# Mixer of a hybrid decoder step: state buffers, turning of the values and head norms rearranged

## The chip, the cores and the metric

The kernel runs on one core of a Trainium2 chip. The metric is the device time of one execution in microseconds (us), lower is better. A core has five engines that work side by side, each through its own list of instructions in order: TensorE (PE, matrix products into PSUM banks; its weight loads are listed as PEld), VectorE (DVE), ScalarE (ACT), GpSimd (POOL) and SyncE (SP, which here only issues transfers). Transfers between the memory (HBM) and the core's buffers (SBUF) are issued by SP or POOL.

## The reference

One inference step of a decoder layer with d = 2048, for a prompt of 256 tokens and 8 samples of 4 tokens each (together T = 288 columns):

```python
x = x + 0.5 * rmsnorm(swiglu(rmsnorm(x, g[0]), ffn1_w_in, ffn1_w_out), g[1])
m, sg, sh = hybrid_mixer(rmsnorm(x, g[2]), ...)
x = x + rmsnorm(m, g[3])
x = x + 0.5 * rmsnorm(swiglu(rmsnorm(x, g[4]), ffn2_w_in, ffn2_w_out), g[5])
```

The mixer projects its input with one matrix into the parts of a GLA group (4 heads, key width 128, value width 256) and an HGRN group (8 heads, 128 and 128). Each head runs the recurrence S_t = diag(a_t) S_{t-1} + k_t^T v_t, o_t = q_t S_t, from zero for the prompt and from a given state for each sample. Each head's output is normalised (rmsnorm), multiplied by silu of a gate, and all heads go through the output projection. The outputs are the new tokens' values, and the states of the prompt and of the samples. Everything is float32.

## The kernel before

The three sub-layers follow each other: FFN1, mixer, FFN2. Activations are kept with features on the 128 partitions and the 288 tokens along the free dimension; a feature tile is 128 x 288. For precision every product is made of three matmuls: a weight is split into wh (ScalarE's rounded copy, L86) and wl (VectorE's rest, L87), an activation into xh and xl, and TensorE adds wh xh (L464), wh xl (L465) and wl xh (L466).

`block` (L455) makes 512 output features: four feature tiles f = 0..3, each with a PSUM bank of its own, over 16 slices k of the input; 192 matmuls in all. After each slice it calls `tick(k)`, which issues a piece of other work into the same in-order lists of the engines; the program's order is the engines' order. The last slices are done tile by tile, and after each tile `evac` takes the bank off. The blocks of the mixer run in the order qk0, v0, qk1, v1 (GLA queries and keys, values, for two pairs of heads), hfq0, hi0, hfq1, hi1, hfq2, hfq3 (HGRN forget gates and queries; values), gate0 to gate3, and the output projection mo0 to mo3.

What `tick` issues comes from generators. `scan` (L764) is one for a pair of heads: eight levels of scores, after which `out`, `final`, `halve`, `sample`, `inter_a`, `inter_b` and `norm_a` follow one step at a time. It holds:
- the samples' states, loaded by SP in `load_state` (L783) into a ring "s0" of four buffers, split by `halve` (L942) into halves hl on ScalarE and VectorE, updated in `sample` (L954) on VectorE (L973) and stored by POOL (L975). A load waits for the store that held its buffer. SP's list holds the loads of weights (L61, L63) and of states in one order;
- the head norm: `norm_a` squares (hsq; the sum of two halves is GpSimd's, L998), `norm_b` (L1006) forms the mean in a scratch bank hms on TensorE, one step later `norm_c` (L1011) takes the inverse root. The list `later` holds how many steps each of these comes behind.

Values are needed with tokens on the partitions. `ev_v` (L741) multiplies a value tile by the row factor into vt (L744, L745), and at once transposes it on TensorE (tp_v, L727 and L728) and copies it to three places (L751, L752, L732 and L734). Such transposes, the scores (sc), out (o, os), sn, st and hms all take their PSUM bank from one ring of three (`auxtile`); the main products have the other five.

`ev_hgrn` (L1114) makes the forget gate, its key k and q from a feature tile z (two buffers) with ScalarE's Exp and Ln; the key's way goes through a tile mx. `ev_gate` (L1170) makes the gate, and for gate0 and gate1 multiplies y by z on GpSimd (L1179).

Of the kernel before, what the change touches and what calls it, by code (L numbers as in the profile page):

```python
# [16 lines left out]
P = 128  # L17
# [98 lines left out]
def trunk_kernel(ctx, tc, x_prompt, x_sample, state_gla, state_hgrn, norm_gains, f1_in, f1_out, f2_in, f2_out,  # L116
# [540 lines left out]
    def mixer(pn, border):  # L657
        with ExitStack() as mx:
# [5 lines left out]
            def scan_pool():  # L664
                border.pools.close()
                sp.append(mx.enter_context(tc.tile_pool(name="scan", bufs=2, side="right", reuse_waits="tile")))
                for i in range(2):
                    its2.append(sp[0].tile([P, 256], F32, name=f"it{i}", bufs=1))
                    vs32.append(sp[0].tile([P, 512], F32, name=f"vs{i}", bufs=1))

                    qm.append(sp[0].tile([P, 9 * 64], F32R, name=f"qm{i}", bufs=1))
            ones = {dv: cst.tile([P, P], F32R, name=f"ones{dv}") for dv in (256, 128)}
            mk = cst.tile([P, 576], U8, name="mk")
            bmask = cst.tile([96, NB], F32, name="bmask")

            sel = cst.tile([P, TS], F32, name="sel")
            its2, vs32, qm = [], [], []
# [7 lines left out]
            def setup():  # L685
# [8 lines left out]
                for t in (*its2, *vs32):  # L694
                    G.memset(t, 0.0)
# [14 lines left out]
                G.tensor_copy(bmask, bm32)  # L710
                for dv in (256, 128):
                    S.activation(ones[dv], onesD, AF.Copy, scale=float(D // dv))
# [28 lines left out]
            def ev_v(Vt, V32, Vs):  # L741
                def ev(f, ps):
                    vt = tmp.tile([P, TP + 96], F32, name="vt", tag="vt")
                    V.tensor_tensor(vt[:, 0:TP], ps[:, 0:TP], rt[:, 0:TP], op=ALU.mult)  # L744
                    V.tensor_tensor(vt[:, TP:].rearrange("p (n t) -> p n t", n=3),  # L745
                                    ps[:, TP:T].unsqueeze(1).broadcast_to([P, 3, TS]),
                                    rt[:, TP:T].unsqueeze(1).broadcast_to([P, 3, TS]), op=ALU.mult)
                    tp = auxtile("tp_v")
                    by_token(tp, vt, vt[:, TP:])
                    c = slice(f * P, (f + 1) * P)  # L750
                    S.activation(Vt[:, 0:2, c], tp[:, 0:TP].rearrange("p (t c) -> p t c", c=P), AF.Copy)  # L751
                    S.activation(V32[0:TS, c], tp[0:TS, TP:TP + P], AF.Copy)  # L752
                    stack(Vs[:, c], tp, TS)
                return ev
# [9 lines left out]
            def scan(d, Vt, V32, Vs, gla, ytile0, s0, sp_out, ss_out):  # L764
# [18 lines left out]
                def load_state():  # L783
                    if loads:
                        a, b0 = loads.pop(0)
                        t = sp[0].tile([P, nb, dv], F32, name="s0", tag="s0", bufs=4)
                        nc.sync.dma_start(t, s0[b0:b0 + nb, a].rearrange("b p v -> p b v"))
                        states[a, b0] = t
# [81 lines left out]
                for step in range(LEVELS + 1):  # L870
# [19 lines left out]
                    if step >= LEVELS - 2:  # L890
                        load_state()
                    yield
                put(LEVELS - 1, pss.pop(LEVELS - 1))
                kds, bds, hls, its, sqs, pos, mss = {}, {}, {}, {}, {}, {}, {}
# [82 lines left out]
                def inter_a(a):  # L977
                    ss = pos[a][1]
                    its[a] = it = its2[a]
                    S.activation(it[0:2 * TS, 0:dv], ss[0:2 * TS, 0:dv], AF.Copy)  # L980
                    if not gla:
                        V.tensor_tensor(it[0:2 * TS, 0:dv], it[0:2 * TS, 0:dv], ss[0:2 * TS, dv:2 * dv], op=ALU.add)

                def inter_b(a):
                    for j in range(nv):
                        c0 = TP + j * TS
                        PE.matmul(pos[a][1][:, c0:c0 + TS], its[a][:, j * P:(j + 1) * P], sel, start=False, stop=True,
                                  skip_group_check=True)

                def norm_a(a):  # L990
                    for j in range(nv):
# [5 lines left out]
                        if j == 1:  # L997
                            G.tensor_tensor(sq, sq, sqs[a], op=ALU.add)  # L998
# [12 lines left out]
                def norm_c(a):  # L1011
                    r0 = tmp.tile([P, T], F32, name="r0", tag="lsg")
                    r1 = tmp.tile([P, T], F32, name="r1", tag="ls")
                    m = tmp.tile([P, T], F32, name="hm", tag="mx")
                    V.tensor_scalar(m, mss[a][:, 0:T], EPS, None, op0=ALU.add)
                    act(r0, m, AF.Ln)
                    act(r0, r0, AF.Exp, scale=-0.5)

                    V.tensor_tensor(r1, r0, r0, op=ALU.mult)
                    V.scalar_tensor_tensor(r1, r1, -0.5, m, op0=ALU.mult, op1=ALU.mult)  # L1020
                    V.scalar_tensor_tensor(r1, r1, 1.5, r0, op0=ALU.add, op1=ALU.mult)
                    for j in range(nv):
                        yt = y[ytile0 + a * nv + j]
                        gcol = prm[:, 108 + j:109 + j] if gla else prm[:, 110:111]
                        V.scalar_tensor_tensor(yt, yt, gcol, r1, op0=ALU.mult, op1=ALU.mult)
# [8 lines left out]
                for a in range(2):  # L1034
# [19 lines left out]
                    later.append([lambda: None, lambda a=a: norm_b(a), lambda a=a: norm_c(a)])  # L1054
# [7 lines left out]
            def tick(k=None):  # L1062

                due = list(later)
                step(k)
# [48 lines left out]
            def ev_hgrn(d, g):  # L1114
                def ev(f, ps):
# [9 lines left out]
                    m = tmp.tile([P, T], F32, name="mx", tag="mx")  # L1125

                    V.tensor_tensor(m, ls, z, op=ALU.subtract)
                    act(m, m, AF.Exp)
                    act(ls, ls, AF.Exp)
                    V.tensor_scalar(d["k"][:, f, :], m, omlb[:, hd:hd + 1], None, op0=ALU.mult)  # L1130
# [21 lines left out]
            for kind, g in HORDER:  # L1152
                if kind == "hi":
                    written(g)
                    vts[g] = vtiles(f"h{g}")
                    block(f"hi{g}", KT, xrhs, ev_v(*vts[g]), tick=tick)
# [13 lines left out]
            def ev_gate(n):  # L1170
                def ev(f, ps):
# [3 lines left out]
                    if n < 2:  # L1175
# [3 lines left out]
                        G.tensor_tensor(y[t], y[t], z, op=ALU.mult)  # L1179
# [96 lines left out]
```

## Time and profile before

| | us |
|---|---|
| three runs | 2312.02, 2314.31, 2318.01 (median 2314.31) |
| profiled execution | 2314.71 |
| its span | 2312.9 |
| TensorE busy | 2291.0 (99%) |
| VectorE, ScalarE, GpSimd busy | 1421.2, 1012.7, 64.4 |
| mixer in the span | 856 to 1448 |
| TensorE's granted clock, mean | 0.997 |

The page gives for each engine the time in which it worked and its share of the span. A group of instructions is written as line, engine, operation, out<-in. A line of waits names who waited, for whom, and then the total, the number of times and the longest, in us. The chain follows the work that ended last back from one instruction to the one that released it; its lines are start, duration and what. Times inside the span are us from its start. The granted clock is the share of full speed at which TensorE was allowed to run.

### The profile page before, as it was taken

The numbers are of one execution on the slowest core, as the hardware profiler recorded it, in microseconds if no ns is written. First come the engines' busy times: TensorE is split into PE (matmuls) and PEld (weight loads), VectorE is DVE, ScalarE is ACT, GpSimd is POOL, SyncE is SP. The second block draws the span as 40 slices with busy tenths as digits, with TensorE's granted clock in tenths as the row PEclk, the third lists the DMA queues.
The fourth block names the chain that finished last, engine by engine and source line by source line (L and its number), as shares of the span: only waits on it lengthen the run. The fifth ranks groups of instructions, "written<-read, shape, count | busy, mean of one in ns | idle before, by whom it ended". The sixth has DMA issues, their size and how long they took to land.

```text
span 2312.9 us, 42140 instructions
## 1 busy us (share of the span) xinstructions
PE 2291.0 (99%) x17352; PEld 2276.1 (98%) x17352; DVE 1421.2 (61%) x2314; ACT 1012.7 (44%) x1555; POOL 64.4 (3%) x110
## 2 busy tenths in 40 slices
PE   9999999999999999999999999999999999999998
PEld 8999999999999999999999999999999999999998
DVE  7545545554556568787889854854555555545545
ACT  6443333333334446454555554544333333333345
POOL 0000000000000001001001100100000000000000
PEclk9999999999999999999999999999999999999999
DMA  7555555555555545555555555455555555555553
GB/s 214 164 166 164 165 166 168 168 165 164 167 167 186 157 151 159 152 152 171 149 169 156 159 184 167 129 160 172 165 165 167 169 164 163 165 164 166 165 164 115
DMA packets 217008, 378.16 MB, mean 163 GB/s; under 512 B 15362, under 2 KB 52400, under 8 KB 216816
## 3 DMA queue, kind: packets, MB, share of 16 engines
q1 hardware_dynamic: 211264, 365.48, 52.6%
q0 software_dynamic: 3376, 9.81, 1.3%
q8 instruction: 136, 2.23, 0.4%
q10 hardware_dynamic: 2176, 0.18, 0.1%
q14 instruction: 56, 0.46, 0.1%
HBM read 363.62 MB, written 11.80 MB: 162 GB/s over the span
## 4 chain that ended last, share of the span: by engine, by line
PE 94%; DVE 3%; issue 1%; DMA 1%; ACT 1%; POOL 0%; DVEq 0%; SPq 0%; POOLq 0%; ACTq 0%
PE gate L465 9%; PE gate L466 9%; PE gate L464 9%; PE out L465 8%; PE out L466 8%; PE out L464 8%; PE up L466 8%; PE up L464 8%; PE up L465 8%; PE hfq L464 2%; PE hfq L465 1%; PE mo L466 1%; PE mo L464 1%; PE mo L465 1%; PE hfq L466 1%; PE sc L830 1%
## 5 line engine op out<-in xcount | busy, mean ns | idle before, releaser
L87 DVE TENSOR_TENSOR wl<-raw,wh 128x1024 fp32r<-128x1024 f32 (+1 forms) x674 | 821.1, 1219 | 629.1 <-ACT wh L86 626.5
L86 ACT ACTIVATE wh<-raw 128x1024 fp32r<-128x1024 f32 (+1 forms) x674 | 711.3, 1056 | 1073.3 <-PE gate L465 323.9
L465 PE MATMUL gate<-xl,wh 128*128 128x288 f32 x1660 | 489.2, 295 | 0.2 <-DVE xl L243 0.2
L464 PE MATMUL gate<-xh,wh 128*128 128x288 f32 x1660 | 488.4, 296 | 0.7 <-DVE z L1174 0.5
L466 PE MATMUL gate<-xh,wl 128*128 128x288 f32 x1660 | 488.7, 295 | 0.2 <-DVE wl L87 0.2
L465 PE MATMUL out<-hl,wh 128*128 128x288 f32 x1408 | 415.8, 295 | 0.0
L464 PE MATMUL out<-hh,wh 128*128 128x288 f32 x1408 | 415.6, 295 | 0.0
L466 PE MATMUL up<-xh,wl 128*128 128x288 f32 x1408 | 415.0, 295 | 0.0
L466 PE MATMUL out<-hh,wl 128*128 128x288 f32 x1408 | 415.0, 295 | 0.0
L464 PE MATMUL up<-xh,wh 128*128 128x288 f32 x1408 | 414.6, 294 | 0.3 <-DVE g L523 0.3
L465 PE MATMUL up<-xl,wh 128*128 128x288 f32 x1408 | 414.8, 295 | 0.0
L465 PEld LDWEIGHTS gate<-xl,wh 128*128 128x128 f32 x1660 | 311.7, 188 | 1.1 <-DVE xl L243 1.0
L464 PEld LDWEIGHTS gate<-xh,wh 128*128 128x128 f32 x1660 | 310.5, 188 | 1.6 <-DVE z L1174 0.7
L466 PEld LDWEIGHTS gate<-xh,wl 128*128 128x128 f32 x1660 | 311.4, 188 | 0.7 <-DVE wl L87 0.7
L466 PEld LDWEIGHTS out<-hh,wl 128*128 128x128 f32 x1408 | 264.7, 188 | 0.0
L464 PEld LDWEIGHTS up<-xh,wh 128*128 128x128 f32 x1408 | 264.1, 188 | 0.6 <-DVE g L523 0.5
L464 PEld LDWEIGHTS out<-hh,wh 128*128 128x128 f32 x1408 | 264.6, 188 | 0.0
L465 PEld LDWEIGHTS out<-hl,wh 128*128 128x128 f32 x1408 | 264.5, 188 | 0.0
L466 PEld LDWEIGHTS up<-xh,wl 128*128 128x128 f32 x1408 | 264.2, 188 | 0.1
L465 PEld LDWEIGHTS up<-xl,wh 128*128 128x128 f32 x1408 | 264.2, 188 | 0.1
L583 DVE TENSOR_TENSOR y<-out,y 128x288 f32<-128x288 f32 x288 | 121.4, 452 | 104.5 <-PE out L466 101.7
L464 PE MATMUL hfq<-xh,wh 128*128 128x288 f32 x256 | 78.7, 307 | 0.0
(342 smaller groups left out, 2581.6 us busy)
## 6 DMA issues: line engine op xcount, KB each, us to landing
raw<-in_ffn_w_in_dram SPq DMA_DIRECT2D x352, 512.0 KB, 3.6
raw<-in_ffn_w_out_dram SPq DMA_DIRECT2D x176, 512.0 KB, 3.7
raw<-in_mix_w_in_dram SPq DMA_DIRECT2D x64, 512.0 KB, 3.7
raw<-in_mix_w_in_dram SPq DMA_DIRECT2D x96, 256.0 KB, 3.3
raw<-in_mix_w_out_dram SPq DMA_DIRECT2D x32, 512.0 KB, 3.8
out_dram<-s POOLq DMA_DIRECT2D x32, 256.0 KB, 3.3
s<-in_state_gla_dram SPq DMA_DIRECT2D x16, 256.0 KB, 3.6
s<-in_state_hgrn_dram SPq DMA_DIRECT2D x16, 256.0 KB, 3.4
```

The lines of the kernel that those rows point to most:

```text
L86: i1 = self.nc.scalar.activation(h[:, c], raw[:, c], AF.Copy).ins
L87: i2 = self.nc.vector.tensor_tensor(l[:, c], raw[:, c], h[:, c].bitcast(F32), op=ALU.subtract).ins
L464: yield lambda: PE.matmul(dst, w[0][:, c:c + P], parts[0], start=start, stop=False)
L465: yield lambda: PE.matmul(dst, w[0][:, c:c + P], parts[1], start=False, stop=False)
L466: yield lambda: PE.matmul(dst, w[1][:, c:c + P], parts[0], start=False, stop=stop)
L583: V.tensor_tensor(y[k], ps, y[k], op=ALU.add)
L830: PE.matmul(ps[0:m, c:c + 64], k[:, a, i * P:i * P + m], r, start=c == 0, stop=True, skip_group_check=True)
```

## The change

Five things, all in the mixer:
- The ring of state buffers "s0" has five buffers, not four, and the loads begin one step earlier (from step LEVELS-3), so they run four ahead. To make place, the two tiles `it` become one, and mx is gone: `ev_hgrn` works in place in z.
- The transposes of the values are no longer issued by `ev_v` itself. It keeps vt in a tile of y that is not yet in use (y[8..11], for hi1 y[12..15]), its samples' part in a small tile v3 (four buffers), and appends a function `turn` to a list. `tick` pops one per step, ahead of the scan's step, except at k = 0. For v0 all four come in qk1's steps 1 to 4; for v1, hi0 and hi1 two come in the block's own last two steps and two in the next block's steps 1 and 2.
- The head norm's `norm_b` and `norm_c` come one step later.
- `norm_c` has a new form: Ln takes EPS as its bias, the square of the inverse root is ScalarE's, and the factor -0.5 lies in a gain made once (hgain). VectorE has two operations per head fewer, ScalarE one more, and the bank hms is read until VectorE's first product.
- The sum of hsq and y times z go from GpSimd to VectorE.

```diff
@@ -664,17 +664,18 @@
             def scan_pool():
                 border.pools.close()
                 sp.append(mx.enter_context(tc.tile_pool(name="scan", bufs=2, side="right", reuse_waits="tile")))
+                its.append(sp[0].tile([P, 256], F32, name="it", bufs=1))
                 for i in range(2):
-                    its2.append(sp[0].tile([P, 256], F32, name=f"it{i}", bufs=1))
                     vs32.append(sp[0].tile([P, 512], F32, name=f"vs{i}", bufs=1))
 
                     qm.append(sp[0].tile([P, 9 * 64], F32R, name=f"qm{i}", bufs=1))
             ones = {dv: cst.tile([P, P], F32R, name=f"ones{dv}") for dv in (256, 128)}
             mk = cst.tile([P, 576], U8, name="mk")
             bmask = cst.tile([96, NB], F32, name="bmask")
+            hgain = cst.tile([P, 3], F32, name="hgain")
 
             sel = cst.tile([P, TS], F32, name="sel")
-            its2, vs32, qm = [], [], []
+            its, vs32, qm = [], [], []
 
             aw, alr = y[KT - 2:], y[KT - 3]
             ahl = gp.tile([P, 32 * KT + 96], F32R, name="ahl", tag="V")
@@ -691,7 +692,7 @@
                 G.dma_start(bm32, masks[0:96, 576:584])
                 for t in (*aw, alr):
                     G.memset(t, 0.0)
-                for t in (*its2, *vs32):
+                for t in (*its, *vs32):
                     G.memset(t, 0.0)
                 for g in range(2):
                     for i in range(2):
@@ -708,6 +709,7 @@
                     G.memset(qm[a].bitcast(F32), 0.0)
                 V.tensor_tensor(sel, ident[:, 0:TS], ident[:, TS:2 * TS], op=ALU.add)
                 G.tensor_copy(bmask, bm32)
+                V.tensor_scalar(hgain, prm[:, 108:111], -0.5, None, op0=ALU.mult)
                 for dv in (256, 128):
                     S.activation(ones[dv], onesD, AF.Copy, scale=float(D // dv))
 
@@ -738,19 +740,26 @@
                 return (gp.tile([P, 2, 512], F32, name=f"V{nm}", tag="V"), vs32[-1],
                         gp.tile([96, 512], F32R, name=f"Vs{nm}", tag="Vs"))
 
-            def ev_v(Vt, V32, Vs):
+            turns = []
+
+            def ev_v(Vt, V32, Vs, y0=8):
                 def ev(f, ps):
-                    vt = tmp.tile([P, TP + 96], F32, name="vt", tag="vt")
+
+                    vt = y[y0 + f]
+                    v3 = tmp.tile([P, 3, TS], F32, name="v3", tag="v3", bufs=4)
                     V.tensor_tensor(vt[:, 0:TP], ps[:, 0:TP], rt[:, 0:TP], op=ALU.mult)
-                    V.tensor_tensor(vt[:, TP:].rearrange("p (n t) -> p n t", n=3),
-                                    ps[:, TP:T].unsqueeze(1).broadcast_to([P, 3, TS]),
+                    V.tensor_tensor(v3, ps[:, TP:T].unsqueeze(1).broadcast_to([P, 3, TS]),
                                     rt[:, TP:T].unsqueeze(1).broadcast_to([P, 3, TS]), op=ALU.mult)
-                    tp = auxtile("tp_v")
-                    by_token(tp, vt, vt[:, TP:])
-                    c = slice(f * P, (f + 1) * P)
-                    S.activation(Vt[:, 0:2, c], tp[:, 0:TP].rearrange("p (t c) -> p t c", c=P), AF.Copy)
-                    S.activation(V32[0:TS, c], tp[0:TS, TP:TP + P], AF.Copy)
-                    stack(Vs[:, c], tp, TS)
+
+                    def turn():
+                        tp = auxtile("tp_v")
+                        by_token(tp, vt, v3.rearrange("p n t -> p (n t)"))
+                        c = slice(f * P, (f + 1) * P)
+                        S.activation(Vt[:, 0:2, c], tp[:, 0:TP].rearrange("p (t c) -> p t c", c=P), AF.Copy)
+                        S.activation(V32[0:TS, c], tp[0:TS, TP:TP + P], AF.Copy)
+                        stack(Vs[:, c], tp, TS)
+
+                    turns.append(turn)
                 return ev
 
             def log_sigmoid(out, z):
@@ -783,7 +792,7 @@
                 def load_state():
                     if loads:
                         a, b0 = loads.pop(0)
-                        t = sp[0].tile([P, nb, dv], F32, name="s0", tag="s0", bufs=4)
+                        t = sp[0].tile([P, nb, dv], F32, name="s0", tag="s0", bufs=5)
                         nc.sync.dma_start(t, s0[b0:b0 + nb, a].rearrange("b p v -> p b v"))
                         states[a, b0] = t
 
@@ -887,11 +896,11 @@
                             S.activation(mh, qa, AF.Copy)
                             V.tensor_tensor(ml, qa, mh.bitcast(F32), op=ALU.subtract)
                             S.activation(K3[:, a], k[:, a, TP:T].unsqueeze(1).broadcast_to([P, 3, TS]), AF.Copy)
-                    if step >= LEVELS - 2:
+                    if step >= LEVELS - 3:
                         load_state()
                     yield
                 put(LEVELS - 1, pss.pop(LEVELS - 1))
-                kds, bds, hls, its, sqs, pos, mss = {}, {}, {}, {}, {}, {}, {}
+                kds, bds, hls, sqs, pos, mss = {}, {}, {}, {}, {}, {}
 
                 def key_t(a):
                     tp = auxtile("tp_k")
@@ -976,7 +985,7 @@
 
                 def inter_a(a):
                     ss = pos[a][1]
-                    its[a] = it = its2[a]
+                    it = its[0]
                     S.activation(it[0:2 * TS, 0:dv], ss[0:2 * TS, 0:dv], AF.Copy)
                     if not gla:
                         V.tensor_tensor(it[0:2 * TS, 0:dv], it[0:2 * TS, 0:dv], ss[0:2 * TS, dv:2 * dv], op=ALU.add)
@@ -984,7 +993,7 @@
                 def inter_b(a):
                     for j in range(nv):
                         c0 = TP + j * TS
-                        PE.matmul(pos[a][1][:, c0:c0 + TS], its[a][:, j * P:(j + 1) * P], sel, start=False, stop=True,
+                        PE.matmul(pos[a][1][:, c0:c0 + TS], its[0][:, j * P:(j + 1) * P], sel, start=False, stop=True,
                                   skip_group_check=True)
 
                 def norm_a(a):
@@ -995,7 +1004,7 @@
                         sq = sqp.tile([P, T], F32, name="hsq", tag="sq")
                         S.activation(sq, yt, AF.Square)
                         if j == 1:
-                            G.tensor_tensor(sq, sq, sqs[a], op=ALU.add)
+                            V.tensor_tensor(sq, sq, sqs[a], op=ALU.add)
                         sqs[a] = sq
                     h = sqp.tile([P, T], F32R, name="nh", tag="pn")
                     l = sqp.tile([P, T], F32R, name="nl", tag="pn")
@@ -1011,18 +1020,16 @@
                 def norm_c(a):
                     r0 = tmp.tile([P, T], F32, name="r0", tag="lsg")
                     r1 = tmp.tile([P, T], F32, name="r1", tag="ls")
-                    m = tmp.tile([P, T], F32, name="hm", tag="mx")
-                    V.tensor_scalar(m, mss[a][:, 0:T], EPS, None, op0=ALU.add)
-                    act(r0, m, AF.Ln)
+                    act(r0, mss[a][:, 0:T], AF.Ln, bias=epst)
                     act(r0, r0, AF.Exp, scale=-0.5)
 
-                    V.tensor_tensor(r1, r0, r0, op=ALU.mult)
-                    V.scalar_tensor_tensor(r1, r1, -0.5, m, op0=ALU.mult, op1=ALU.mult)
-                    V.scalar_tensor_tensor(r1, r1, 1.5, r0, op0=ALU.add, op1=ALU.mult)
+                    S.activation(r1, r0, AF.Square)
+                    V.scalar_tensor_tensor(r1, mss[a][:, 0:T], EPS, r1, op0=ALU.add, op1=ALU.mult)
+                    V.scalar_tensor_tensor(r1, r1, -3.0, r0, op0=ALU.add, op1=ALU.mult)
                     for j in range(nv):
                         yt = y[ytile0 + a * nv + j]
-                        gcol = prm[:, 108 + j:109 + j] if gla else prm[:, 110:111]
-                        V.scalar_tensor_tensor(yt, yt, gcol, r1, op0=ALU.mult, op1=ALU.mult)
+                        V.scalar_tensor_tensor(yt, yt, hgain[:, j:j + 1] if gla else hgain[:, 2:3], r1,
+                                               op0=ALU.mult, op1=ALU.mult)
 
                 tp = key_t(0)
                 halve(0, 0)
@@ -1051,7 +1058,7 @@
                     yield
                     inter_b(a)
                     norm_a(a)
-                    later.append([lambda: None, lambda a=a: norm_b(a), lambda a=a: norm_c(a)])
+                    later.append([lambda: None, lambda: None, lambda a=a: norm_b(a), lambda a=a: norm_c(a)])
                     yield
                     if a == 0:
                         out(1)
@@ -1062,6 +1069,8 @@
             def tick(k=None):
 
                 due = list(later)
+                if turns and k != 0:
+                    turns.pop(0)()
                 step(k)
                 for f in due:
                     f.pop(0)()
@@ -1122,12 +1131,11 @@
                         V.scalar_tensor_tensor(d["q"][:, f - 2, :], z, QSCALE, ls, op0=ALU.mult, op1=ALU.mult)
                         return
                     hd = 2 * g + f
-                    m = tmp.tile([P, T], F32, name="mx", tag="mx")
-
-                    V.tensor_tensor(m, ls, z, op=ALU.subtract)
-                    act(m, m, AF.Exp)
+
+                    V.tensor_tensor(z, ls, z, op=ALU.subtract)
+                    act(z, z, AF.Exp)
                     act(ls, ls, AF.Exp)
-                    V.tensor_scalar(d["k"][:, f, :], m, omlb[:, hd:hd + 1], None, op0=ALU.mult)
+                    V.tensor_scalar(d["k"][:, f, :], z, omlb[:, hd:hd + 1], None, op0=ALU.mult)
                     V.tensor_scalar(d["f"][:, f, :], ls, omlb[:, hd:hd + 1], lb[:, hd:hd + 1], op0=ALU.mult, op1=ALU.add)
                 return ev
 
@@ -1153,7 +1161,7 @@
                 if kind == "hi":
                     written(g)
                     vts[g] = vtiles(f"h{g}")
-                    block(f"hi{g}", KT, xrhs, ev_v(*vts[g]), tick=tick)
+                    block(f"hi{g}", KT, xrhs, ev_v(*vts[g], 8 + 4 * g), tick=tick)
                 else:
                     written(g)
                     ds[g] = group_tiles(f"h{g}")
@@ -1176,7 +1184,7 @@
                         s = tmp.tile([P, T], F32, name="lsg", tag="lsg")
                         log_sigmoid(s, z)
                         act(s, s, AF.Exp)
-                        G.tensor_tensor(y[t], y[t], z, op=ALU.mult)
+                        V.tensor_tensor(y[t], y[t], z, op=ALU.mult)
                     else:
                         s = z
                         act(z, z, AF.Silu)
```

## The prediction

> **What bounds the kernel now.** I read the page's busy table first, then the groups of matmuls, then the waits of TensorE, and last the chain, the waits and the clock of the one stretch where TensorE stood longest.
>
> ```profile
> PE 2291.0 (99%) x17352; PEld 2276.1 (98%) x17352; DVE 1421.2 (61%) x2314; ACT 1012.7 (44%) x1555; POOL 64.4 (3%) x110
> L464 PE MATMUL hfq<-xh,wh 128*128 128x288 f32 x256 | 78.7, 307 | 0.0
> ```
>
> TensorE (PE) is the bound from end to end; VectorE (DVE) at 61% and ScalarE (ACT) at 44% have room as averages, and GpSimd (POOL) does almost nothing. A matmul of 128x288 is listed with some 295 to 307 ns, but they overlap: in the chain below one follows the other every 0.13 us (132 ns). The change removes no matmul, so all that it can take away is time in which TensorE waits or runs slowly:
>
> ```profile
> PE tp_prm L269 <- DMA stage<-in_norm_gains_dram: 4.7, 1, 4.7
> PE tp_v L728 <- DVE vt L745: 3.3, 1, 3.3
> PE pre L353 <- DVE acc L326: 0.7, 2, 0.5
> PE sc L830 <- DVE k_h L813: 0.7, 1, 0.7
> PE hms L1009 <- ACT nh L1002: 0.5, 1, 0.5
> PE gate L464 <- DVE z L1174: 0.5, 1, 0.5
> PE tp_v L727 <- DVE vt L744: 0.4, 1, 0.4
> PE tp_v L727 <- DVE Vsg L734: 0.3, 1, 0.3
> ```
>
> Columns: total, times, longest, in us. The first and third are outside the mixer and stay. The others, 5.7 us, are all at places that the change touches. The 3.3 us is one event, at the border from block hi0 to block hfq1. The chain there:
>
> ```profile
> 1061.48 3.52 DMA out_dram<-s
> ...
> 1065.02 3.44 DMA s<-in_state_hgrn_dram
> ...
> 1068.50 1.05 ACT wh L86
> ...
> 1069.57 1.23 DVE wl L87
> 1070.80 0.18 DVE vt L745
> ...
> 1071.02 0.45 PE tp_v L728
> ```
>
> Read it upwards: the transpose of the values waits for vt, which stands in VectorE's order behind the rounding rest wl of a weight, that behind ScalarE's wh, and wh stands in ScalarE's order behind the copy hl of a state that had not landed; the state's load had waited for a buffer that an older state's store still held. The waits of 1050 to 1075 us agree:
>
> ```profile
> ACT hl L950 <- DMA s<-in_state_hgrn_dram: 5.9, 2, 3.0
> DVE wl L87 <- ACT wh L86: 5.8, 2, 3.6
> ```
>
> And what comes after the stop (columns: stretch, length, busy of PE, PEld, DVE, ACT, POOL, granted clock, DMA share, GB/s):
>
> ```profile
> 1066.00:1071.00 5.00, 1.73 (x14) 1.50 (x12) 1.43 (x4) 1.67 (x3) 0.00 (x0) 0.93 0.56 174
> 1071.00:1078.00 7.00, 6.98 (x35) 6.93 (x36) 4.79 (x14) 3.95 (x15) 0.95 (x1) 0.57 0.65 187
> 1078.00:1085.00 7.00, 7.00 (x64) 6.74 (x63) 6.18 (x15) 2.70 (x7) 0.13 (x1) 1.00 0.07 10
> ```
>
> In the 7 us behind the stop TensorE is busy throughout but was granted 0.57 of its clock: 35 matmuls where the next 7 us hold 64. That is 7 x 0.43 = 3.0 us lost on top of the wait.
>
> **The change, part by part.** Sum against the profiled execution, 2314.71 us (span 2312.9 and 1.8 around it), 0.4 us above the median of 2314.31. Stalls are counted from start to start of TensorE's instructions in the trace, as excess over the same pair elsewhere, so they come out some tenths above the listed waits. 0.3%, about what a measurement of this kernel can tell from no change, is 6.9 us.
>
> *The stop at 1071 us (five state buffers, turns later).* It takes 3.45 us of wait and 3.0 us of half clock, 6.45 us. In the new order ScalarE still has wh behind the copy of the second HGRN state. But with a fifth buffer that load waits for the store before the one it waited for: that store landed at 1061.1 us, the one waited for now at 1062.1. So the load takes the place in SP's queue of the first HGRN load, issued at 1061.2 and landed at 1064.1 (2.9 us), where the second was issued at 1062.2 and landed at 1068.1 (5.9 us). Then three copies hl and it (0.3 us apart), wh 1.05 us to about 1066.2, wl 1.23 us to about 1067.5, and the two halves of the value's product (0.41 and 0.25 us) to about 1068.0; the last main matmul of hi0 is at 1067.6. Left: about 0.4 us, without a clock loss, as stops of under 1 us show none (below). Gain 6.05 us. If the load still takes 5.9 us, the stop stays as it is: gain 0. If there were no wait at all, 6.45. I take 6.05: 2.9 us is the row of the load issued at that time.
>
> The queues passed: SP issues the HGRN loads one place earlier, ahead of weight loads (hgrn1 before the weights that it followed). The weights behind a load that waits for its buffer wait as well; the store that hgrn1 needs landed at 1051.6 us, so it doesn't block, and the pair of weights behind hgrn2 and hgrn3 goes out at about 1063 as before. POOL's stores are moved past nothing.
>
> *The border v1 to hfq0, 993 to 999 us.* Three stops: 0.61 us (tp_v for vt), 0.48 us (tp_v for its bank, held by Vsg), 0.70 us (hms for nh): 1.79 us. The first two come from ScalarE, which at 986.0 to 989.8 us stands 3.9 us for a state's load, with the copy hl (0.40), wh (0.96), wl (1.23) and vt (0.34) in line behind. With the fifth buffer this load is issued several us earlier. The hms stop ends with hsq on POOL (1.35 us) and nh (0.45 us); one step more is 12 main matmuls, 1.6 us, over twice the stop. I leave 0.2 us: gain 1.6 (0 to 1.8).
>
> *Gates, 1259.0, 1293.8 and 1297.0 us.* 0.88 us (sc for k), 0.67 us (the next gate's bank for z on VectorE) and 0.30 us (hms). There POOL's y x z takes 0.80 to 1.0 us, once 3.06 us, and VectorE's products beside it take 0.92 and 1.06 us against 0.44 alone. On VectorE y x z costs 0.44 us each, 8 x 0.44 = 3.5 us in all, less than the slowed neighbours cost. The order of TensorE's instructions also puts the score about 8 and the gate's next block about 7 main matmuls later (0.9 us). Gain 0.9 + 0.9 = 1.8 us (0 to 1.85).
>
> *Head norms.* 12 heads lose two VectorE operations each (hm and the square, 24 x 0.45 = 10.8 us busy) and give ScalarE one Square (12 x 0.43 = 5.2 us); the four adds of hsq come to VectorE (4 x 0.41 us) with the eight y x z. Net VectorE -5.7 us of 1421, ScalarE +5.2 of 1013. Neither is on the path: 0, hidden by TensorE's main matmuls (192 in a block, 25.4 us). If the cover is gone one norm costs its own 0.4 us.
>
> *What is new.* The gate z is now overwritten in place, so its buffer is held through two exponentials until k is made, about 1.3 us longer than when mx took it; the third feature tile's z needs the buffer of the first, and frees the bank that the next block wants. The bank of hfq3's fourth tile is claimed at 1187.64 us, 0.08 us after z frees one: no slack. By the order of VectorE's work I put 0.15 us at hi0, 0.3 at hfq3, 0.3 at gate0. The four turns of hi1 now share three scratch banks with out and sn at the start of hfq2: 0.1. Together 0.85 us; bounds 0 (the tenths are free) and 4 x 0.88 = 3.5 us (the dearest short stop of the trace at each of the four).
>
> Sum: -6.05 - 1.6 - 1.8 + 0.85 = -8.6 us: 2314.71 - 8.6 = **2306.1 us**.
>
> **A rule weighed.** The trace's row: a stop of 3.45 us, then 6.1 us at half the clock; the stops of 0.3 to 0.9 us were followed by none. The Trainium skill, "TensorE: Matmul & The Clock Gate", section "Part 1: The HAM clock gate", says that the clock halves after an idle window of about 3.4 us which runs free of the kernel. By that rule 3.45 us would only just, and in few executions, hold a whole window, so that some runs before had no loss; after the change nothing that long is left in the mixer and the forecast time is the same by rule and by row. The lowest run of before, 2312.02 us, is 2.7 us below the profiled one, which would fit. The gain against such a run would be 5.6 us.
>
> **The rivals.**
> - *The load stays slow (0.15).* Loads and stores of 256 KB took 2.5 to 5.9 us to land; around 1063 to 1069 us the queue holds two stores, three state loads and two weights. If hgrn2 again takes 5.9 us, TensorE stands about 3.1 us and loses the 3.0 us as now: 2306.1 + 6.05 = 2312.2 us. For it: the same transfers still collide. Against: the load issued at 1061.2 took 2.9.
> - *The half clock stays (0.08).* If it comes from something other than the stop: 2306.1 + 3.0 = 2309.1 us. Against: no other place in the mixer shows it.
> - *The short stops stay (0.10).* Of the 3.4 us at v1 and the gates nothing goes, as other work in the same in-order queues takes the place: 2309.5 us. That the fifth buffer and the later turns do nothing there belongs here.
> - *Slower: scratch banks (0.12).* An hms bank is now held until VectorE's first product, with Ln, Exp and Square (3 x 0.43 us) on ScalarE before it, possibly behind one wh (1.06) and two hl (2 x 0.36), and that product (0.45) behind one wl (1.22): 4.7 us. There are three banks; a third claim after hms comes about two steps later, 3.2 us. TensorE would then stand 1.5 us in each of 12 norms, 18 us: 2324 us. It turns the sign from (8.2 + 6.9) / 12 = 1.3 us a norm. Against: rarely do all stand in line, and ScalarE is at 44%.
>
> **How the numbers follow.** The forecast has 0.55, its own range 2303.5 (all stops gone, nothing new: 2314.71 - 10.1 = 2304.6, and run to run about 1) to 2309. Faster by 0.3% means below 2307.4, of which I give it 0.43, and 0.02 to gains not seen: 0.45. Slower is the bank rival, 0.12. The rest, 0.43, is within 0.3%. The range 2303 to 2315 holds all but the bank rival and a little below.
>
> **What would show it.** Right: no wait of TensorE above 1 us in the mixer, clock 1.00 just behind hi0, no wait of ScalarE's hl on the HGRN loads beyond 1 us, POOL without products. Wrong: a tp_v that waits 3 us for y at the same border; or waits at claims of scratch banks (sc, sn, tp_k) on r1; or a gate or hfq first matmul that waits for z.

## The result and the profile after

The changed kernel took 2305.85 us (median of 6 runs, 2304.71 to 2306.81), the kernel before 2314.48 us (median of 6, 2312.02 to 2318.01): ratio 0.9965, 95% interval 0.9955 to 0.9975. It is faster by 0.35%, just over what can be told from no change. The profiled execution took 2305.61 us with a span of 2303.8, against 2314.71 and 2312.9.

The page's busy table after:

```profile
PE 2287.0 (99%) x17352; PEld 2274.0 (99%) x17352; DVE 1415.0 (61%) x2303; ACT 1018.9 (44%) x1567; POOL 50.8 (2%) x97
```

The number of matmuls is the same. VectorE has 6.2 us less work and ScalarE 6.2 us more (put at 5.7 and 5.2); both were hidden, as said. The waits of TensorE (total, times, longest, us):

```profile
PE tp_prm L269 <- DMA stage<-in_norm_gains_dram: 4.6, 1, 4.6
PE tp_v L729 <- DVE y L750: 0.8, 1, 0.8
PE pre L353 <- DVE acc L326: 0.7, 2, 0.5
PE v L464 <- DVE k_g L1100: 0.4, 1, 0.4
```

Of the six kinds of waits in the mixer that the change touches, one is left: the transpose at the end of hi0 (now L729) still waits, 0.8 us where it was 3.3. Besides, the wait of v for k_g in block v0 is 0.4 us, where it was 0.2. The chain at hi0's end, in the changed kernel:

```profile
1055.07 4.07 DMA out_dram<-s
...
1059.20 3.17 DMA s<-in_state_hgrn_dram
...
1062.47 0.12 ACT hl L959
...
1063.46 0.96 ACT wh L86
...
1064.45 0.94 DVE wl L87
...
1065.59 0.43 DVE y L750
...
1066.06 0.44 PE tp_v L729 x2
```

It has the same links as before: a store, the load into its buffer, ScalarE's hl and wh, VectorE's wl and the value, the transpose. But the load, the second of the HGRN states, goes out at 1059.2 us and takes 3.2 us, where it took 5.9. ScalarE still waits for it:

```profile
ACT hl L959 <- DMA s<-in_state_hgrn_dram: 3.4, 1, 3.4
```

And the clock behind the stop is whole (columns as in the table of stretches before: stretch, length, five engines, granted clock, DMA share, GB/s):

```profile
1066.00:1071.00 5.00, 4.94 (x41) 4.94 (x42) 4.88 (x15) 2.78 (x12) 0.00 (x0) 1.00 0.79 209
1071.00:1078.00 7.00, 7.00 (x64) 6.77 (x63) 6.08 (x17) 3.72 (x10) 0.00 (x0) 1.00 0.36 103
```

To see where the time went, I counted main matmuls in both traces and took the time from the mixer's first one to the last one of each block. Difference to the kernel before, in us, one profiled execution each (e1, e9 and e10 are experiments told of below):

| up to the end of | after | e1: loads alone | e10: loads and VectorE | e9: six buffers, norm at the old step |
|---|---|---|---|---|
| v1 | +0.07 | 0.00 | 0.00 | +0.13 |
| hfq0 | -2.03 | -1.50 | -1.74 | -1.89 |
| hfq1 | -6.92 | -6.66 | -7.26 | -7.69 |
| hfq3 | -6.39 | -6.68 | -7.31 | -7.91 |
| gate0 | -6.55 | -6.70 | -7.33 | -7.94 |
| gate1 | -7.23 | -6.69 | -8.48 | -8.89 |
| gate2, and the mixer's end | -8.30 | -6.68 | -9.76 | -9.99 |

The remaining 0.8 us between the two profiled executions (9.1 in all) lie outside the mixer, where the kernels are the same.

### The profile page after: what moved, and what is told of

Same layout as the page of the kernel before. It is cut to its first block, busy times and chain, and to the rows that moved or that the text cites. A ratio compares the mean times of both kernels' runs of the same rounds, so it can differ in the third digit from the quotient of the medians.

```text
span 2303.8 us, 42125 instructions
## 1 busy us (share of the span) xinstructions
PE 2287.0 (99%) x17352; PEld 2274.0 (99%) x17352; DVE 1415.0 (61%) x2303; ACT 1018.9 (44%) x1567; POOL 50.8 (2%) x97
## 4 chain that ended last, share of the span: by engine, by line
PE 88%; issue 7%; DVE 2%; DMA 1%; POOL 1%; ACT 1%; DVEq 0%; POOLq 0%; ACTq 0%; SPq 0%
PE gate L464 9%; PE gate L466 9%; PE gate L465 9%; PE out L465 8%; PE out L466 8%; PE out L464 8%; PE up L466 8%; PE up L464 8%; PE up L465 8%; PE mo L466 1%; PE mo L464 1%; PE mo L465 1%; PE hfq L464 1%; PE hfq L465 1%; PE hfq L466 1%
```

## The experiments

In the table, "mixer" is the length of the stretch from the first qk matmul's start to the last mo matmul's start in the profile, against 591.0 us before; one execution each. The ratio is to the kernel before, run on the same chip in the same turn. Times from different chips differ by a microsecond even for the kernel before (2313.35, 2314.65, 2313.48 and 2313.77 us), so differences of less are read from the traces alone.

| kernel | us, median (lowest to highest) | ratio, 95% interval | mixer |
|---|---|---|---|
| the change | 2305.85 (2304.71 to 2306.81) | 0.9965 (0.9955 to 0.9975) | 582.7 |
| e1 loads alone | 2308.23 (2307.66 to 2308.79) | 0.9980 (0.9971 to 0.9989) | 584.3 |
| e2 loads undone | 2309.76 (2307.87 to 2313.44) | 0.9987 (0.9978 to 0.9996) | 590.0 |
| e3 turns undone | 2307.16 (2306.13 to 2308.28) | 0.9974 (0.9964 to 0.9984) | 583.7 |
| e4 norm at the old step | 2305.26 (2304.01 to 2305.63) | 0.9958 (0.9945 to 0.9970) | 581.6 |
| e5 GpSimd back | 2305.75 (2305.15 to 2305.86) | 0.9966 (0.9954 to 0.9979) | 582.5 |
| e7 six buffers | 2306.07 (2305.54 to 2306.88) | 0.9963 (0.9949 to 0.9977) | 581.8 |
| e9 six buffers, norm at the old step | 2305.07 (2304.62 to 2305.34) | 0.9964 (0.9951 to 0.9976) | 581.0 |
| e10 loads and VectorE | 2304.22 (2303.83 to 2304.81) | 0.9960 (0.9947 to 0.9974) | 581.3 |
| e11 loads and norm | 2306.47 (2305.91 to 2306.87) | 0.9971 (0.9959 to 0.9982) | 582.6 |
| e12 buffer without early loads | 2307.40 (2306.16 to 2307.85) | 0.9971 (0.9960 to 0.9982) | 582.4 |

**e1: the loads alone.** To the kernel before:

```diff
-                    its2.append(sp[0].tile([P, 256], F32, name=f"it{i}", bufs=1))
+                its2.extend([sp[0].tile([P, 256], F32, name="it", bufs=1)] * 2)
-                        t = sp[0].tile([P, nb, dv], F32, name="s0", tag="s0", bufs=4)
+                        t = sp[0].tile([P, nb, dv], F32, name="s0", tag="s0", bufs=5)
-                    if step >= LEVELS - 2:
+                    if step >= LEVELS - 3:
```

> The kernel before with the fifth state buffer and the loads one step earlier, nothing else of the change (the two tiles it become one, to make the space). Theory, loads: the stop at hi0's end was set by the state's load alone, so TensorE's wait there falls from 3.45 us to 1 us or less, the clock just behind it is 1.00, the two tp_v stops at 993 and 996 us go (1.1 us), the hms stops (0.7 and 0.3 us) and the gate stops (0.88 and 0.67 us) stay: 2307.5 to 2308.5 us, about 6.5 us under before. Rival, turns: the transposes issued at once by the value block are what makes TensorE wait; the stop shrinks by less than 1.5 us and the half clock stays: 2311 us or more.

Measured 2308.23 us. The stop at hi0's end is 0.28 us from start to start, the clock behind it whole, the two tp_v stops at 993 and 996 us are gone. TensorE's waits in this kernel show what the loads do not touch:

```profile
PE sc L830 <- DVE k_h L813: 0.7, 1, 0.7
PE hms L1009 <- ACT nh L1002: 0.7, 2, 0.4
PE gate L464 <- DVE z L1174: 0.5, 1, 0.5
```

So the buffers carry 6.7 of the mixer's 8.3 us (by the medians 5.1 of 8.6 us), with the transposes left where they were. The rival, that the place of the transposes makes the stop, is out.

**e2: the loads undone.** To the changed kernel: four buffers, and `step >= LEVELS - 2`.

```diff
-                        t = sp[0].tile([P, nb, dv], F32, name="s0", tag="s0", bufs=5)
+                        t = sp[0].tile([P, nb, dv], F32, name="s0", tag="s0", bufs=4)
-                    if step >= LEVELS - 3:
+                    if step >= LEVELS - 2:
```

> The changed kernel with four state buffers and the loads started at the old step. Theory, loads: the stop at hi0's end comes back with 3 us or more, and if it is as long as before, the half clock behind it too: 2309 us (stop alone) to 2313 us (stop, half clock, and the v1 border). Rival, turns: with the transposes in the next block's steps TensorE has other work, and the time stays at 2306 us.

2309.76 us, and runs that lie 5.6 us apart. In the profile TensorE stops at both borders again, 1.9 us at 993.6 and 2.85 us at 1072.3 us, and again ScalarE waits for loads. The waits of 1050 to 1076 us, and then the stretches around both stops:

```profile
ACT hl L959 <- DMA s<-in_state_hgrn_dram: 6.0, 2, 4.8
PE tp_v L730 <- DVE v L751: 2.7, 1, 2.7
```

```profile
992.00:995.00 3.00, 1.39 (x12) 1.40 (x13) 3.00 (x10) 2.35 (x6) 0.72 (x1) 1.00 0.66 194
995.00:999.00 4.00, 4.00 (x22) 3.97 (x21) 2.63 (x7) 2.57 (x11) 0.00 (x0) 0.57 0.66 202
999.00:1003.00 4.00, 4.00 (x33) 4.00 (x33) 3.46 (x8) 2.19 (x7) 0.00 (x0) 1.00 0.34 115
1070.00:1074.00 4.00, 1.67 (x14) 1.68 (x15) 3.12 (x9) 3.42 (x10) 0.00 (x0) 0.99 0.30 82
1074.00:1077.50 3.50, 3.50 (x18) 3.50 (x17) 1.94 (x5) 1.20 (x5) 0.00 (x0) 0.53 1.00 277
```

That was new: a stop of only 1.9 us is followed by half the clock too, but for a shorter time. The records of the granted clock say for how long: 3.41 us from 995.39, 3.41 us from 1073.90; in the kernel before it was 6.83 us from 1070.26. That led to e6 and e8.

**e12: the buffer without the early loads.** Which half of "loads" does it? To the changed kernel, `step >= LEVELS - 2` alone.

```diff
-                    if step >= LEVELS - 3:
+                    if step >= LEVELS - 2:
```

> The changed kernel with its five state buffers, but the loads start at the old step, so that only three run ahead. Theory, place in the order: the fifth buffer alone gives little, since each load is still issued one halving later, when the buffer that it could have had has long been free; the second HGRN load comes as late as with four buffers and the stop of 2 to 3 us at hi0's end is back, with a half clock of one or two windows in some executions: 2308.5 to 2310 us. Rival, buffer: the load was late only for the store that it waited for, and a fifth buffer removes that wait wherever the load stands: 2306 us, no stop above 1 us.

2307.40 us; mixer 582.4. My theory falls: in the changed kernel the buffer alone is enough. (On the kernel before, it was not tried alone.) The second HGRN load went out at 1061.6 us and landed in 3.0 us; ScalarE waits as long as in the changed kernel, and TensorE's stop there is 0.7 us:

```profile
ACT hl L959 <- DMA s<-in_state_hgrn_dram: 3.2, 1, 3.2
```

The early step's worth isn't seen in this trace. e2 and e12 differ in one buffer: 7.6 us of mixer in the profiles, 2.4 us in the medians of runs (the profiled execution of e2, span 2311.7, holds the half clock twice and is the longest of its runs). All 11 runs of e2 lie above all 7 of e12.

**e3: the turns undone.** To the changed kernel:

```diff
-                    turns.append(turn)
+                    turn()
```

> The changed kernel with each value tile's transposes issued at once in its evacuation, as before. Theory, loads: the turns carry little; TensorE waits 0.3 to 1 us more in all at the ends of v1, hi0 and hi1: 2306 to 2307.5 us. Rival, turns: each of the three borders waits 0.5 to 1 us more for its four tiles: 2308 to 2309 us.

2307.16 us, mixer 1.0 us longer: the turns are worth about one microsecond, within what the theory that they carry little gave. The stop at hi0's end was 1.1 us from start to start; 0.3 us are at hfq2's start (o); none of the others that the change did not have is above 0.25 us (sn at 1043.4 has 0.3 in both).

**e4 and e9: the norm at the old step.** To the changed kernel; e9 has the sixth buffer of e7 too.

```diff
-                    later.append([lambda: None, lambda: None, lambda a=a: norm_b(a), lambda a=a: norm_c(a)])
+                    later.append([lambda: None, lambda a=a: norm_b(a), lambda a=a: norm_c(a)])
```

> The changed kernel with the mean and the end of the head norm one step earlier, as before. Theory: the hms waits of 0.7 us (hfq0) and 0.3 us (gate2) come back at most, though the sum of hsq on VectorE is shorter than on GpSimd: 0.3 to 1.0 us more, 2306 to 2307 us. Rival, scratch banks: the banks of hms held long are what little is lost now, and the time falls by 0.5 us or more.

> The changed kernel with six state buffers (loads one step earlier still) and the head norm at the old step: the two variations that took a stop of TensorE away or cost nothing. Theory: no stop above 0.6 us is left in the mixer, 2305 us, 0.5 to 1 us under the change, at the limit of what is told from no change. Rival: the same as the change, 2306 us.

e4 took 2305.26 us with a mixer 1.1 us shorter; no hms wait came back. Of the 1.1 us, 0.75 are there at hfq1's end already, since this execution had no stop at hi0's end. e9 took 2305.07, its mixer 0.8 us shorter than that of e7, which differs only in the step. The hms waits that the later step was to remove are already gone with the sum of hsq on VectorE (e10, at the old step, has none either); the later step itself loses 0.4 us by e4 and 0.8 us by e9 against e7, one execution each. That it is the scratch bank of hms, as my rival had it, was not shown.

**e5: GpSimd back.** To the changed kernel:

```diff
-                            V.tensor_tensor(sq, sq, sqs[a], op=ALU.add)
+                            G.tensor_tensor(sq, sq, sqs[a], op=ALU.add)
-                        V.tensor_tensor(y[t], y[t], z, op=ALU.mult)
+                        G.tensor_tensor(y[t], y[t], z, op=ALU.mult)
```

> The changed kernel with the eight products y x z and the four sums of hsq on GpSimd again. Theory: the score's wait for k (0.9 us) and the gate's wait for z (0.7 us) come back wholly or in part, and hms waits for nh now find a step of 1.6 us more, so they stay away: 2306.5 to 2307.5 us. Rival: the new order of TensorE's instructions alone took these stops, GpSimd had no part: 2306 us, and no wait of TensorE above 0.3 us in the gates.

2305.75 us, the same as the change. In the trace two stops are back at gate2's start, 0.67 us (the bank that z frees) and 0.30 us (hms); the wait for z and GpSimd's work there:

```profile
PE gate L464 <- DVE z L1182: 0.5, 1, 0.5
```

```profile
1280.05 3.81 POOL L1187 TENSOR_TENSOR y<-y,z 128x288 f32<-128x288 f32 x2 [2.91 <-DVE z L1182]
1284.82 0.95 POOL L1187 TENSOR_TENSOR y<-y,z 128x288 f32<-128x288 f32 x1 [0.96 <-DVE z L1182]
```

The score's stop of 0.88 us did not come back. The one microsecond lost at the gates is not in the total, since this execution had no stop at hi0's end (0.94 us in the change's).

**e10 and e11: a second part beside the loads.** Both to e1. e10 moves y x z and the sum of hsq to VectorE (the edit of e5, reversed). e11 takes the norm's new form, a step later (`norm_c` and `later` as in the change, the gain scaled in place); turns, GpSimd and mx stay as before.

> The kernel before with the fifth buffer and earlier loads, and y x z and the sum of hsq on VectorE; turns and norm as before. Theory: of the six stops that the loads alone left in the mixer (0.53, 0.28, 0.48, 0.88, 0.67 and 0.32 us, 3.15 us) the gates' z and hms (0.67, 0.32) go, and the hms stops at the starts of hfq0 and hfq1 shrink, as VectorE's add is shorter than GpSimd's: 2306.5 us, 1.5 us under the loads alone. The score's stop of 0.88 us stays, since it did not come back with GpSimd. Rival: GpSimd had a part in that one too and it goes: 2305.8 us.

> The kernel before with the fifth buffer and earlier loads, and the head norm in its new form and a step later; turns, GpSimd and mx as before. Theory: the hms stops (0.53, 0.48 and 0.32 us) go, and with two VectorE operations fewer in each norm the score at gate0's end has its k sooner, so 0.88 us goes too: 2306 to 2306.5 us. Rival: the norm takes only the hms stops, the score's stop comes from the order of the turns or of z: 2307 us.

e10 took 2304.22 us, less than either figure expected. Its mixer is 3.1 us shorter than that of e1, and the score's stop of 0.88 us went as well, as the rival had it. The hms, gate and sc waits are all gone; the only wait of TensorE above 0.3 us that is left from v1 on is, at hi0's end,

```profile
PE tp_v L727 <- DVE vt L744: 0.4, 1, 0.4
```

e11 took 2306.47 us; its mixer is 1.7 us shorter than that of e1. The score's stop went here too, and the hms stop at hfq1; the one at hfq0 stayed (0.53 us, now ahead of its second matmul), and so did the two at gate2's start (0.67 and 0.31). So the score's stop is cured by either part. Each takes time off VectorE ahead of the score, which would explain it, but no run shows that this is the reason. The two at gate2 go only where the products and the sums leave GpSimd; which of these two moves does it was not separated. Two of the five parts of the change, the buffers and the move to VectorE, do all that the whole does, and 1.5 us of mixer more. Its median is the lowest of all (by ratio e4's is), but its interval overlaps the change's, so that it beats the change too is told by one trace of each, not by the times.

**e7: six buffers.** To the changed kernel: `bufs=6` and `step >= LEVELS - 4`.

```diff
-                        t = sp[0].tile([P, nb, dv], F32, name="s0", tag="s0", bufs=5)
+                        t = sp[0].tile([P, nb, dv], F32, name="s0", tag="s0", bufs=6)
-                    if step >= LEVELS - 3:
+                    if step >= LEVELS - 4:
```

> The changed kernel with a sixth state buffer and the loads one step earlier still. Theory: ScalarE's wait of 3.4 us for the second HGRN state goes, and with it the 0.9 us in which TensorE still waits at the end of hi0: 2305 us, 0.9 us under the change. Rival: the earlier load stands before weights in SP's queue, and the load of a later state waits for its store there; a weight comes late and the time is 2306 us or more.

2306.07 us: no gain in the time. In the trace the stop at hi0's end is gone and the mixer is 0.9 us shorter, but as e4 and e5 had no stop there either with five, the 0.9 us is not the sixth buffer's alone. This one is open.

**e6 and e8: stops on purpose.** Both are the changed kernel with stops of TensorE in the FFN blocks c >= 1, at k = 6:

```diff
+    def stop(k):
+        if k != 6 or not lengths:
+            return
+        t0 = auxtile("stop0")
+        PE.transpose(t0[:, 0:P], ident, ident)
+        V.tensor_copy(dummy, t0[:, 0:P])
+        for _ in range(lengths.pop(0)):
+            V.tensor_tensor(dummy, dummy, ident, op=ALU.add)
+        t1 = auxtile("stop1")
+        PE.transpose(t1[:, 0:P], dummy, ident)
```

> The changed kernel with 38 stops of TensorE put into the middle of FFN blocks: a transpose, a chain of dependent VectorE adds of a length between 4 and 34, and a transpose that waits for it; stops of about 1.2 to 8 us, each length twice, in scattered order. Nothing is left out of the computation. Theory, length: every stop above about 3.4 us is followed by some 6 us at half the clock, a loss of 3 us, and no stop below it by any. Theory, free window: a stop loses clock only if a whole window of about 3.4 us falls into it, so stops of 3.5 us nearly never do, those of 5 us about every second time, and those of 6.8 us and more always; two stops of one length may differ. Time in all by the length theory about 2306 + 38 x 4 + 18 x 3 = 2510 us, by the window theory about 2490 us.

e6 took 2342.32 us and told nothing of long stops: TensorE worked on through the chains and waited at most 1.2 us. A scheduler, which puts the program's instructions into the engines' lists, had moved the next main matmuls ahead of the second transpose (15 to 131 matmuls stand between the two in the trace); so what I wrote above, that the program's order is the engines' order, holds only as far as that scheduler keeps it. It shows one thing: 35 waits of up to 1.2 us lost no clock. The mixer of e6 is that of the change, and yet its tp_v at hi0's end waits 1.9 us, without losing clock; there the second HGRN load goes out 1.1 us later, counted from the mixer's start. In e8 the wait is 1.7 us. With the 0.8 us of the change and none in e4, e5 and e7, what is left of this stop varies from execution to execution. e8 holds the order by hand:

```diff
-                for ready in mm3(ps[f][:, 0:T], w, f, k, rhs(k), k == 0, k == nk - 1):
-                    ready()
+                with ExitStack() as es:
+                    for i in held:
+                        es.enter_context(tc.issue_after(i))
+                    for ready in mm3(ps[f][:, 0:T], w, f, k, rhs(k), k == 0, k == nk - 1):
+                        ready()
```

> As the kernel with 38 stops, but each later main matmul is now kept behind the stop's second transpose, so that nothing fills the stop; VectorE's chains have 2 to 19 adds (0.325 us each in the run before), stops of some 1.5 to 7 us. Nothing is left out. The two half clocks of the kernel with four buffers began on a grid of 3.41 us and lasted one window each, though its stops were only 1.9 and 2.9 us. Theory, share of a window: the grid runs free, and a window in which TensorE idles more than a share between 0.3 and 0.5 is followed by a window at half the clock, a loss of 1.7 us; stops of 1.5 to 3 us lose or not by where they fall, stops over 3.4 us always lose. Theory, whole window: only a window that is idle from end to end counts; stops under 3.4 us never lose. Theory, length: every stop over one fixed length loses, whatever its place. Time about 2306 + 38 x 3.6 + some 35 windows x 1.7 = 2500 us by the first, 2460 us by the second.

2519.94 us. There are 40 stops (not 38), 1.5 to 7.0 us long, together 143.5 us:

```profile
PE stop L512 <- DVE dummy L510: 143.5, 40, 7.0
```

All records of the granted clock in this kernel begin on one grid of 3.41 us; between the first and the last stop 41 windows were at half the clock, 139.9 us. In 24.5 us of these TensorE stood in one of the stops, so the half clock cost half of the other 115.4 us, 57.7 us. From the main matmul before a stop to the one after it there are, without the listed wait and the usual step, 0.37 us more for the added transposes, 14.8 us in all. 2306 + 143.5 + 57.7 + 14.8 = 2522.0 us, 2 us above the time measured. Two stops of the same length, 2.40 us, at 251.0 and at 1788.7 us, each shown by the two windows of the grid that it touches:

```profile
250.69:254.11 3.42, 1.02 (x9) 0.77 (x8) 2.63 (x8) 0.00 (x0) 0.00 (x0) 1.00 0.56 176
254.11:257.52 3.41, 3.41 (x17) 3.41 (x16) 0.47 (x1) 1.06 (x1) 0.00 (x0) 0.50 0.06 22
1786.69:1790.11 3.42, 1.96 (x15) 1.70 (x14) 2.07 (x5) 1.06 (x1) 0.00 (x0) 1.00 0.48 153
1790.11:1793.52 3.41, 2.47 (x19) 2.47 (x20) 0.98 (x4) 0.65 (x1) 0.00 (x0) 1.00 0.49 154
```

The first lies in one window, of which TensorE worked 1.02 us: the next window runs at 0.50, 17 matmuls where 26 or so fit. The second is split over two windows that keep 1.96 and 2.47 us of work: nothing is lost. By all 40: none of 4 stops of up to 1.8 us lost clock, 8 of 15 between 2.07 and 3.11 us did, all 21 from 3.42 us on. The theory of a share holds, though the share here is above the 0.3 to 0.5 that it gave (see the last section); those of a length and of a wholly idle window are out.

## Why the prediction was right

*The stop at hi0's end (predicted -6.05, with +0.15 for the new wait there).* Right in mechanism and in place: the load that ScalarE waits for has 2.9 us in the forecast and 3.17 us in the trace, and no clock was lost. From hfq0's end to hfq1's end the trace has -4.9 us. The load line in the chain that I showed (1065.02, 3.44) is not that load: by the trace the one issued at 1065.02 landed at 1070.9, after the copy hl had begun at 1068.18. The sum used the right one (1062.2 to 1068.1). The term mis-sized is "about 0.4 us left": it was 0.94 us. I had kept the end of hi0 at 1067.6 us, but the gain at v1 brought it forward to 1065.0, by 2.6 us, and the load by only 2.0: here the chain behind the transfer did not move up as far as TensorE's work. One sign that I gave for being right failed: ScalarE's hl waits 3.4 us for the load, not 1 us at most. What became shorter is the load, and with it TensorE's wait at the end of the chain.

*The half clock (3.0 of it).* Right that it came from the stop, and that stops under 1 us lose none; the rival that it stays is out (e1, e2, e8). But I took one execution's loss for a fixed cost. By e8 a stop of 3.4 us is followed by one window at half the clock at least, 1.7 us; the profile of before shows two. Its runs lie 6.0 us apart, those of the change 2.1. So the gain by profiles is 9.1 us, by medians 8.6.

*v1's border (-1.6).* -2.1 us; e1 shows that the loads alone bring 1.5 of it.

*The gates (-1.8).* -1.75 us from gate0's end to gate2's. The reason was half right: the move off GpSimd took the waits at gate2's start (e5, e10, e11). For the score I credited the new order of TensorE's instructions; e10 and e11 have the old order of the turns and lose the stop too.

*New waits (0.85, of which 0.15 is counted at hi0 above).* 0.4 us: 0.07 up to v1's end, 0.37 from hfq1's end to gate0's. I had put them on z's buffer, held longer. e9 has z in place as well and shows none there (-7.69 to -7.94), so z alone does not make them. e7, which differs from e9 only in the norm's later step, loses 0.40 us there; but e4, at the old step, loses 0.28, and e11, with the later step and without z in place and the turns, gains 0.28. So the later step, which I had counted as a gain and otherwise free, has a part in them together with other parts of the change, and which is open. This is the step whose reason was not borne out; its size is within what I gave.

*The rivals.* The load that stays slow: the load took 3.2 us, not 5.9. The scratch banks: TensorE's waits name no bank in the scan; one sn starts 0.3 us late, which e4, e7 and e9 put down to VectorE's ks and not to a bank. That the short stops at v1 and the gates stay: none of them did. (Of the two waits of pre, which I had put outside the mixer, one of 0.3 us, at 905 us, lies in it; it stayed.)

The sum, -8.6 us, met the medians' -8.6. Against the profiles the misses were +1.0 at hi0, -0.5 at v1, -0.3 in the new waits and +0.05 at the gates, which gives the mixer's -8.3; that they cancel so well is luck.

## What to carry to other kernels

Where one engine is busy 99% of the time, look for the few places where it stops, and follow each chain back to its transfer; here one more buffer in a ring of four carried most of the gain of a change in five parts. Parts that cure the same wait do not add up, so try them singly: two of the five gave all of it, and one (the later norm), by the traces, took a little back. Then count a stop of the tensor engine not by its length alone, but with the clock behind it.

## What the hardware showed that was not expected

The clock of TensorE was granted in windows of 3.41 us on a grid that runs free of the kernel: in e6 and e8 TensorE starts at 4.66 us, but the grid's lines lie 1.8 us apart (first records at 10.16 and 8.35 us). With idle time taken between the recorded end of a matmul and the start of the next, in the FFN of e8 a full-speed window in which TensorE idled 58% or more was always followed by one at half the clock, and one with up to 55% never; in the mixer of e2 windows with 48% and 54% idle were, and in that of e6 one with 46% was not. In the mixer transposes and small products filled part of the rest; that this makes the difference is not shown. A half-speed window was followed by another one if TensorE idled in it 22% or more (before and e8), and by a full one with 18% or less. So a stop of 1.9 us (e2) cost 1.7 us more, and one of 3.4 us 1.7 us (e8) or 3.0 us (before) by where it fell. That may be one source of the spread of the runs before, of which only one was profiled.

The Trainium skill, "TensorE: Matmul & The Clock Gate", section "Part 1: The HAM clock gate", has the window's length and the free grid as these traces do; where it asks for an idle window, these runs show that about half of one is enough.
